# A decoder layer on one core: squares of token group 2 moved into the down stage, first loads and last output in smaller parts, late weight loads reordered

## The chip, the cores and the metric

The kernel runs on one core of a Trainium2 chip. The core has five engines with instruction queues of their own: TensorE (PE: matmuls; its weight loads are shown apart as PEld), VectorE (DVE), ScalarE (ACT), GpSimd (POOL) and SyncE (SP), which here issues nearly all DMAs. Each engine works through its queue in order and waits on semaphores for the others. TensorE writes to the eight banks of PSUM; DVE and ACT read them and so make them free again. The metric is the time of one execution in microseconds (us), the median of several runs. All durations below come from one profiled execution.

## What is computed

One layer of a decoder for 1024 prompt tokens and 32 decode tokens, D = 1024, all in float32. Cut to what matters:

```python
h = rms(x, n_mix_pre)
z = h @ w_in                                  # q | k | v | pooling input
mix = concat(attention(z), pooling(z)) @ w_out
x = x + rms(mix, n_mix_post)
f = rms(x, n_ffn_pre)
f = (silu(f @ w_gate) * (f @ w_up)) @ w_down  # 2816 hidden channels
x = x + rms(f, n_ffn_post)
x = x + sigmoid(x @ w_ple_gate) * (p @ w_ple) # the output y
```

`rms(a, g)` is `a * rsqrt(mean(a*a) + eps) * g` over the 1024 channels.

## The kernel before

**Tiles.** The 1056 tokens are three groups (0, 1, 2) of 352. Channels lie on the 128 partitions, tokens on the columns; the 1024 channels are 8 chunks `m` of 128. Almost every matmul is 128x128 weights against 128x352 columns.

**Precision by pairs.** Each float32 operand is split into a rounded high part and the rest: ACT casts (`wh`, `qh`, `sh`, L167), DVE subtracts (`wl`, `ql`, `sl`, L168). `gemm` (L367) makes three matmuls of each product: high by high, high by low, low by high. So TensorE can use no weight before ACT and then DVE have split it. The pairs of weights share the eight slots of `w_tile` (L180); raw weights have three slots, tag "wr" (`W_RAW`, L52); everything as large as half a group lives in 28 activation slots (`act_tile`, L110, `A_SLOTS`); small results such as `sg`, `yo`, `u3` have five slots (`tmp`, L133).

**Seven products instead of eight.** Groups 0 and 1 are multiplied together by Strassen's scheme: sums of weight blocks (POOL, L328 for the down weights, L1128 in `w_sums` for the others) meet sums of activations. Group 2 is multiplied directly. The sums overwrite the raw weights, so the plain split of a raw tile has to come before its sums.

**The order.** TensorE's instructions keep the order in which the program text issues them (`mm`, L124). The other engines' instructions are put in order by the planner of the framework, by their place in the text and by when it reckons them ready; `fix`, `order` and `load` pin single ones. Weights are made ready ahead of use: `need(k)` (L330) walks a list `ITEMS`, makes what is up to `LOOK` = 4 items ahead (split, or sums and split) but none from `until[0]` on, and asks for the raw weights of the next two items by `w_load` (L172).

**Side chains.** Norms run as generators beside the matmuls. `turn(n)` (L972) counts matmuls; `chain(steps, wait)` (L985) lets a generator make its first step `wait` matmuls later, and further steps as the counter passes the times that the generator's own loads set. `rstd_steps` (L391) turns a sum of squares `acc` into a broadcast 1/rms, with six small matmuls, a square root on ACT, a few DVE operations and two matmuls. `ple_steps(g)` (L1332) loads `p` and the saved residual `x1d`, runs `rstd_steps(acc3[g], 28)`, scales, adds and splits the result for the last stage.

**The stages the change touches.**
- Start: `u_load`, `x_load` (L458 on) issue the first weights and x on SP; `u_split`, `x_operand` split them; `u_prod` multiplies, for all four weight tiles first half of the channels, then second half. `x_squares` and `sum_halves` make the sum of squares of x, and `rstd_steps` of group 0 comes after the eighth `u_prod`.
- Output projection: `out_attn(m, g)` for the first four chunks and `out_proj(m, g)` for the last four (groups 0 and 1 here; group 2 is done). `ffn_steps(2)` (L995) is chained ahead of them and makes group 2's norm, residual sum, second norm and operand for the hidden layers. `turn(12)` stands behind each `out_attn`, `turn(24)` behind each `out_proj`.
- Down: `gate_up` and `down` (L1210) run over the hidden slabs; after the last slab `downs(LAST2, (0, 1))` makes the last eight down products of group 2 and, behind each, `finished(m, 2)` (L1233): square on ACT, add into `acc3[2]` on DVE, scale by the gain on ACT. Then `down7(n)` (L1257) runs 19 steps of the Strassen products of groups 0 and 1; each of the steps 0 to 11 is 48 matmuls. `ple_steps(2)` is chained in front of the first step with `wait` 110.
- Last stage: `ple_out(m, 2)` for group 2, then for groups 0 and 1 `ple_first(a)` for a = 7, 5, 3, 1 (a first product, kept as `p1` by ACT, L1443, then a second onto the same bank) and `ple_rest(a, b)` for the pairs (1,0), (3,2), (5,4), (7,6): products with one "half" item and one "sums" item of weights each, added by DVE (L1454). `ple_end` (L1406) makes sigmoid (ACT, L1410), product and sum (DVE, L1412, L1414) and stores the output on SP (L1415).

Of the kernel before, what the change touches and what calls it, by code (L numbers as in the profile page):

```python
# [10 lines left out]
F32 = mybir.dt.float32  # L11
F32R = mybir.dt.float32r
AF = mybir.ActivationFunctionType
# [12 lines left out]
N = T // G  # L26
# [35 lines left out]
def trunk_kernel(  # L62
# [43 lines left out]
    def nm(s):  # L106
        cnt[0] += 1
        return f"{s}{cnt[0]}"
# [4 lines left out]
    def half(g, dt=F32, s="h"):  # L113
        return act_tile([P, 4, NS[g]], dt, s)
# [54 lines left out]

    raws, pairs = {}, {}  # L170

    def w_load(j):  # L172
        if j >= len(plan) or j in raws:
            return
        src, shape = plan[j]
        t = wpool.tile(shape, F32, tag="wr", bufs=W_RAW, name=nm("wr"))
        nc.sync.dma_start(t, src)
        raws[j] = t

# [267 lines left out]
    def load(dst, src):  # L447
        tc.keep_in_program_order(nc.sync.dma_start(dst, src))
# [18 lines left out]
    def x_operand(g, h, behind=False):  # L467
        t = xr[g, h]
        hi, lo = half(g, F32R), half(g, F32R)
        for c in range(4):  # L470
            gc = gn[:, 0, 4 * h + c : 4 * h + c + 1]
            fix(se.activation(hi[:, c, :], t[:, c, :], AF.Identity, scale=gc))  # L472
# [4 lines left out]
        xs[g][h] = hi, lo  # L477

    def x_squares(g):
        sqs = [xr[g, h] for h in range(2)]  # L480
# [2 lines left out]
        acc1[g] = sum_halves(sqs, g)  # L483


    def u_load(c, h):
        j = U0[c]
        if h == 0:
            shape = plan[j][1]
            raws[j] = act_tile(shape) if c == 3 else wpool.tile(shape, F32, tag="wr", bufs=W_RAW, name=nm("wr"))  # L490
        load(raws[j][:, 4 * h : 4 * h + 4, :], plan[j][0][:, 4 * h : 4 * h + 4, :])

    def u_split(c, h):
        j = U0[c]
        if h == 0:
            pairs[j] = w_tile(plan[j][1], "wh"), w_tile(plan[j][1], "wl")
        split(*(t[:, 4 * h : 4 * h + 4, :] for t in pairs[j]), raws[j][:, 4 * h : 4 * h + 4, :])

    u_load(0, 0)
    x_load(0, 0, 2)  # L500
    for c in range(1, 4):
        u_load(c, 0)
    x_load(0, 1)
# [874 lines left out]
    for k in OPERAND.values():  # L1378
        spill(k, len(SETS) - 1)
    share[0] = 0.3  # L1380
    chain(ple_steps(2), 110)
    for n in range(len(STEPS) - 2):
        down7(n)
    finish(list(chains))

    early = {}
# [16 lines left out]
        se.copy(v, embed(wp, m, g))  # L1403
        early[m, g] = v

    def ple_end(gate, wp, m, g):  # L1406

        pp = early.pop((m, g)) if (m, g) in early else embed(wp, m, g)
        sg = tmp(N, "sg")
        se.activation(sg, gate, AF.Sigmoid)  # L1410
        xm = x2[g][m // 4][:, m % 4, :]
        ve.tensor_tensor(sg, sg, pp, op=ALU.mult)  # L1412
        yo = tmp(N, "yo")
        ve.tensor_tensor(yo, sg, xm, op=ALU.add)  # L1414
        nc.sync.dma_start(y_o[:, m, OFF[g] : OFF[g + 1]], yo)  # L1415

    def ple_out(m, g):
        wp, w = WPE[0][m]
# [30 lines left out]
    def ple_rest(a, b):  # L1449
        wp, w, js = W2[a]  # L1450
        p1 = p1s[0][:, a // 2, :]

        def add(out, x, ps):
            ve.tensor_tensor(out, x, ps, op=ALU.add)  # L1454
# [24 lines left out]
    chain(ple_steps(0), 84)  # L1479
    down7(len(STEPS) - 2)  # L1480
# [9 lines left out]
    for a, b in zip(firsts, firsts[1:] + [()]):  # L1490
# [4 lines left out]
        list(a)  # L1495
    finish(list(chains))
    for a, b in PAIRS:
        ple_rest(a, b)
# [86 lines left out]
```

## Time and profile before

| | us |
|---|---|
| median of 3 runs | 1093.62 (1093.57 to 1094.39) |
| profiled execution | 1093.46 |
| its span, first to last instruction | 1091.7 |
| POOL adding down weights, L328, 44 instructions | 72.9 |
| POOL adding other weights, L1128, 52 instructions | 78.9 |

How to read the rows: the view of waits has engine, line, whom it waited for, then us in total, times, and the longest. A row of windows has the window's limits and length, then each engine's busy time with its count of instructions, the granted TensorE clock (1.00 is full), the share of the time in which the 16 DMA engines were busy, and GB/s. A row of the timeline has start, duration, engine, line, operation, output<-inputs, shapes and count; behind it in brackets stands how long the engine had been idle before and who ended that. A row of groups has the count, then busy time, mean ns of one, and idle time before them. Tile names carry no numbers, so "p" is `p1`, "sh" the high part of a sum of weights, "st" a staged activation, "xo" one that is loaded back.

### The profile page before, as it was taken

Reading aid. Unit: us, or ns where it says so; the run is one execution under the profiler, and the core shown is the slowest. Engines: PE = TensorE matmul, PEld = TensorE weight load, DVE = VectorE, ACT = ScalarE, POOL = GpSimd, SP = SyncE. Lnnn points to the kernel's source line nnn. Section 1 sums busy time; section 2 is a strip of 40 time slices with the busy share of each in tenths; the row PEclk is TensorE's granted clock in tenths of the full one; section 3 lists DMA queues with packets and bytes.
Section 4 is the critical chain, followed back from the end, with each engine's and each line's share of the span. In section 5 each row is a group of like instructions: output and inputs, shape, how many; then the busy total and the mean of one; then the engine's idle time right before and its main releaser. Section 6 shows DMA issues by size and latency. Waiting matters only on the chain.

```text
span 1091.7 us, 17619 instructions
## 1 busy us (share of the span) xinstructions
PE 1076.9 (99%) x6867; PEld 1058.8 (97%) x6867; DVE 822.1 (75%) x1277; ACT 512.0 (47%) x921; POOL 279.3 (26%) x213
## 2 busy tenths in 40 slices
PE   9999999999999999999999999999999999999997
PEld 8999988899999999999999999999998999999996
DVE  6766378976888966867758758659669767999877
ACT  8322277764555534344334434435356532575442
POOL 1045023200000042322423223242409085200242
PEclk9999999999999999999999999999999999999998
DMA  8121211352543312342441523515777855837241
GB/s 295 59 71 39 95 61 40 131 226 69 205 172 116 120 54 68 141 184 84 142 180 58 209 112 111 229 39 184 286 261 300 334 176 180 316 116 235 85 148 61
DMA packets 54452, 163.60 MB, mean 150 GB/s; under 512 B 5828, under 2 KB 20068, under 8 KB 54368
## 3 DMA queue, kind: packets, MB, share of 16 engines
q1 hardware_dynamic: 53040, 160.70, 41.8%
q10 hardware_dynamic: 1328, 1.77, 0.5%
q8 instruction: 54, 0.88, 0.3%
q14 instruction: 30, 0.25, 0.1%
HBM read 124.59 MB, written 37.86 MB: 149 GB/s over the span
## 4 chain that ended last, share of the span: by engine, by line
PE 93%; DVE 3%; ACT 1%; issue 1%; DMA 1%; POOL 0%; ACTq 0%; SPq 0%; DVEq 0%; POOLq 0%
PE b L126 93%; PE b L120 1%; DMA xr<-in_x_dram 0%; POOL wr L1128 0%; ACT a L742 0%; DVE yo L1414 0%; DMA wr<-in_w_in_dram 0%; ACT wh L167 0%; DVE u L1329 0%; DVE sg L1412 0%; DVE p L1454 0%; DVE wl L168 0%; DVE ql L168 0%; DVE st L168 0%; DVE u L1454 0%
## 5 line engine op out<-in xcount | busy, mean ns | idle before, releaser
L126 PE MATMUL b<-fh,wh 128*128 128x352 f32 x712 | 229.9, 323 | 0.7 <-ACT p L1443 0.7
L126 PE MATMUL b<-fh,wl 128*128 128x352 f32 x712 | 228.3, 321 | 0.0
L126 PE MATMUL b<-fl,wh 128*128 128x352 f32 x712 | 228.1, 320 | 0.0
L1128 POOL TENSOR_TENSOR wr<-wr 128x512 f32<-128x512 f32 x52 | 78.9, 1517 | 561.2 <-DVE wl L168 275.8
L168 DVE TENSOR_TENSOR wl<-wr,wh 128x1024 fp32r<-128x1024 f32 (+1 forms) x125 | 164.2, 1315 | 57.5 <-ACT wh L167 56.4
L167 ACT CAST wh<-wr 128x1024 fp32r<-128x1024 f32 (+1 forms) x125 | 128.2, 1028 | 153.1 <-PE b L126 98.6
L126 PE MATMUL b<-xo,qh 128*128 128x352 f32 x616 | 147.4, 322 | 0.5 <-DVE o L1225 0.5
L126 PE MATMUL b<-fh,sh 128*128 128x352 f32 x416 | 135.0, 325 | 2.0 <-DVE p L1454 2.0
L126 PEld LDWEIGHTS b<-fh,wh 128*128 128x128 f32 x712 | 133.5, 188 | 1.0 <-ACT p L1443 1.0
L126 PEld LDWEIGHTS b<-fl,wh 128*128 128x128 f32 x712 | 133.9, 188 | 0.0
L126 PE MATMUL b<-fh,sl 128*128 128x352 f32 x416 | 133.8, 322 | 0.0
L126 PE MATMUL b<-fl,sh 128*128 128x352 f32 x416 | 133.8, 322 | 0.0
L126 PEld LDWEIGHTS b<-fh,wl 128*128 128x128 f32 x712 | 133.4, 187 | 0.3 <-DVE wl L168 0.2
L126 PEld LDWEIGHTS b<-xo,qh 128*128 128x128 f32 x616 | 106.6, 188 | 0.8 <-DVE o L1225 0.8
L126 PE MATMUL b<-h,wh 128*128 128x352 f32 x480 | 105.7, 326 | 1.3 <-ACT h L472 0.9
L126 PE MATMUL b<-xo,ql 128*128 128x352 f32 x308 | 99.4, 323 | 2.0 <-DVE ql L168 1.9
L168 DVE TENSOR_TENSOR sl<-wr,sh 128x1024 fp32r<-128x1024 f32 x52 | 63.4, 1220 | 42.3 <-ACT sh L167 42.2
L328 POOL TENSOR_TENSOR wq<-wq,wq 128x512 f32<-128x512 f32 x44 | 72.9, 1695 | 71.3 <-DVE ql L168 60.1
L126 PEld LDWEIGHTS b<-h,wh 128*128 128x128 f32 x480 | 82.5, 190 | 2.2 <-ACT h L472 1.1
L126 PE MATMUL b<-hid,wh 128*128 128x352 f32 x352 | 84.1, 322 | 0.0
L167 ACT CAST sh<-wr 128x1024 fp32r<-128x1024 f32 x52 | 53.6, 1049 | 63.0 <-POOL wr L1128 59.1
L167 ACT CAST st<-c 128x352 fp32r<-128x352 f32 x55 | 26.7, 487 | 117.6 <-DVE c L1199 96.7
(202 smaller groups left out, 2176.6 us busy)
## 6 DMA issues: line engine op xcount, KB each, us to landing
wr<-in_w_gu_dram SPq DMA_DIRECT2D x64, 512.0 KB, 3.4
xd<-st SPq DMA_DIRECT2D x35, 704.0 KB, 4.5
xo<-xd SPq DMA_DIRECT2D x35, 704.0 KB, 6.0
wr<-in_w_dn_dram SPq DMA_DIRECT2D x22, 512.0 KB, 3.5
wq<-in_w_dn_dram SPq DMA_DIRECT2D x20, 512.0 KB, 8.9
wr<-in_w_pg_dram SPq DMA_DIRECT2D x18, 512.0 KB, 3.9
x<-in_x_dram SPq DMA_DIRECT2D x6, 704.0 KB, 9.0
x1d<-x SPq DMA_DIRECT2D x6, 704.0 KB, 3.6
```

Of the source, the lines that this page charges most:

```text
L120: ins = te.transpose(out, src, ident)
L126: ins = te.matmul(*args, **kw)
L167: fix(se.copy(hi, src))
L168: fix(ve.tensor_tensor(lo, src, hi.bitcast(F32), op=ALU.subtract))
L328: ge.tensor_tensor(*(q_load(q, e)[:, i, :] for q in (out, a, b)), op=op)
L1128: ge.tensor_tensor(out, a, b, op=op)
```

## The change

1. First loads: the first chunk (of eight) of the first w_in tile is a transfer of its own, then the first chunk of x, then chunks 1 to 3 of the weights, then x in one and two chunks. It was four chunks of weights, then x by two and two. The splits follow the same parts.
2. `finished(m, 2)` is no longer called behind each last down product, but two at a time after `down7(2)` to `down7(5)`; `ple_steps(2)` is chained after step 5 with `wait` 40.
3. In the last stage `until[0]` is set to the first "sums" item, so that none is made before the last `ple_first` has begun; at that point it is lifted, and the raw weights of the three later pairs are asked for at once, those of the last two pairs into activation slots.
4. The norm chain of group 2 ahead of the hidden layers, `ffn_steps(2)`, is chained with `wait` 16, where it was 8.
5. `ple_end` can work in parts: the last output adds, takes the sigmoid, multiplies, adds and stores in two halves of 176 columns.

```diff
-    def w_load(j):
+    def w_load(j, home=None):
...
-        t = wpool.tile(shape, F32, tag="wr", bufs=W_RAW, name=nm("wr"))
+        t = home(shape) if home else wpool.tile(shape, F32, tag="wr", bufs=W_RAW, name=nm("wr"))
...
-    def x_load(g, h, n=1):
+    def x_load(g, h, parts=(4,), behind_first=None):
         xr[g, h] = half(g, s="xr")
-        for c in range(0, 4, 4 // n):
-            cs = slice(c, c + 4 // n)
-            k = slice(4 * h + c, 4 * h + c + 4 // n)
-            load(xr[g, h][:, cs, :], x[:, k, OFF[g] : OFF[g + 1]])
+        c = 0
+        for n in parts:
+            load(xr[g, h][:, c : c + n, :], x[:, 4 * h + c : 4 * h + c + n, OFF[g] : OFF[g + 1]])
+            if c == 0 and behind_first:
+                behind_first()
+            c += n
...
-    u_load(0, 0)
-    x_load(0, 0, 2)
+    u_part(0, slice(0, 1))
+    x_load(0, 0, (1, 1, 2), lambda: u_part(0, slice(1, 4)))
...
-    u_split(0, 0)
-    x_operand(0, 0)
+    u_split(0, 0, slice(0, 1))
+    x_operand(0, 0, cs=range(1))
+    u_split(0, 0, slice(1, 4))
+    x_operand(0, 0, cs=range(1, 4))
...
-    chain(ffn_steps(2), 8, alone=True)
+    chain(ffn_steps(2), 16, alone=True)
...
                 down(n, m)
-                if n == LAST2:
-                    finished(m, 2)
...
-    chain(ple_steps(2), 110)
     for n in range(len(STEPS) - 2):
         down7(n)
+        if 2 <= n < 6:
+            for m in (2 * n - 4, 2 * n - 3):
+                finished(m, 2)
+        if n == 5:
+            chain(ple_steps(2), 40)
...
-    def ple_end(gate, wp, m, g):
+    def ple_end(gate, wp, m, g, parts=1, into=None):
...
+        n = N // parts
+        for i in range(0, N, n):
+            v = slice(i, i + n)
+            if into is not None:
+                ve.tensor_tensor(into[:, v], into[:, v], gate[:, v], op=ALU.add)
+            se.activation(sg[:, v], (gate if into is None else into)[:, v], AF.Sigmoid)
+        for i in range(0, N, n):
+            v = slice(i, i + n)
+            ve.tensor_tensor(sg[:, v], sg[:, v], pp[:, v], op=ALU.mult)
+            ve.tensor_tensor(yo[:, v], sg[:, v], xm[:, v], op=ALU.add)
+            nc.sync.dma_start(y_o[:, m, OFF[g] + i : OFF[g] + i + n], yo[:, v])
...
-        if not early_s4:
-            add(p1, p1, product(s["S4"], e7["B22"]))
-        ple_end(p1, wp, a, 1)
+        if early_s4:
+            ple_end(p1, wp, a, 1)
+        else:
+            ple_end(product(s["S4"], e7["B22"]), wp, a, 1, parts=2, into=p1)
...
     finish(chains[:-1])
+    until[0] = W2[1][2]
     firsts = [ple_first(a) for a in (7, 5, 3, 1)]
...
         if not b:
+            until[0] = len(ITEMS)
+            for a, _ in PAIRS[1:]:
+                for j in ITEMS[W2[a][2]][1]:
+                    w_load(j, act_tile if a > 4 else None)
             for m in range(4):
                 embed_early(W1[1][0], m, 1)
```

The `u_part` helper loads any chunks of a w_in tile, and `u_split` and `x_operand` take the chunks to split.

More of the change, by code (lines that the diff above doesn't have):

```diff
@@ L456, in trunk_kernel, with x_operand @@
     xr = {}
-    def x_load(g, h, n=1):
+    def x_load(g, h, parts=(4,), behind_first=None):
         xr[g, h] = half(g, s="xr")
-        for c in range(0, 4, 4 // n):
-            cs = slice(c, c + 4 // n)
-            k = slice(4 * h + c, 4 * h + c + 4 // n)
-            load(xr[g, h][:, cs, :], x[:, k, OFF[g] : OFF[g + 1]])
+        c = 0
[4 more added lines that the diff above has]
+            c += n
     xs, acc1, r1 = [[None] * 2 for _ in range(G)], [None] * G, [None] * G
-    def x_operand(g, h, behind=False):
+    def x_operand(g, h, behind=False, cs=range(4)):
         t = xr[g, h]
-        hi, lo = half(g, F32R), half(g, F32R)
-        for c in range(4):
+        hi, lo = xs[g][h] = xs[g][h] or (half(g, F32R), half(g, F32R))
+        for c in cs:
             gc = gn[:, 0, 4 * h + c : 4 * h + c + 1]
@@ L483, in x_squares, with u_part, u_load, u_split @@
         acc1[g] = sum_halves(sqs, g)
-    def u_load(c, h):
+    def u_part(c, ks):
         j = U0[c]
-        if h == 0:
+        if j not in raws:
             shape = plan[j][1]
             raws[j] = act_tile(shape) if c == 3 else wpool.tile(shape, F32, tag="wr", bufs=W_RAW, name=nm("wr"))
-        load(raws[j][:, 4 * h : 4 * h + 4, :], plan[j][0][:, 4 * h : 4 * h + 4, :])
-    def u_split(c, h):
+        load(raws[j][:, ks, :], plan[j][0][:, ks, :])
+    def u_load(c, h):
+        u_part(c, slice(4 * h, 4 * h + 4))
+    def u_split(c, h, part=slice(0, 4)):
         j = U0[c]
-        if h == 0:
+        ks = slice(4 * h + part.start, 4 * h + part.stop)
+        if j not in pairs:
             pairs[j] = w_tile(plan[j][1], "wh"), w_tile(plan[j][1], "wl")
-        split(*(t[:, 4 * h : 4 * h + 4, :] for t in pairs[j]), raws[j][:, 4 * h : 4 * h + 4, :])
-    u_load(0, 0)
-    x_load(0, 0, 2)
+        split(*(t[:, ks, :] for t in pairs[j]), raws[j][:, ks, :])
+    u_part(0, slice(0, 1))
+    x_load(0, 0, (1, 1, 2), lambda: u_part(0, slice(1, 4)))
     for c in range(1, 4):
@@ L1404, in embed_early @@
         early[m, g] = v
-    def ple_end(gate, wp, m, g):
+    def ple_end(gate, wp, m, g, parts=1, into=None):
         pp = early.pop((m, g)) if (m, g) in early else embed(wp, m, g)
-        sg = tmp(N, "sg")
-        se.activation(sg, gate, AF.Sigmoid)
         xm = x2[g][m // 4][:, m % 4, :]
[L1412 to L1415, printed above, removed]
+        sg, yo = tmp(N, "sg"), tmp(N, "yo")
+        n = N // parts
[9 more added lines that the diff above has]
+            nc.sync.dma_start(y_o[:, m, OFF[g] + i : OFF[g] + i + n], yo[:, v])
     def ple_out(m, g):
@@ L1487, in trunk_kernel @@
     finish(chains[:-1])
+    until[0] = W2[1][2]
     firsts = [ple_first(a) for a in (7, 5, 3, 1)]
     next(firsts[0])
-    for a, b in zip(firsts, firsts[1:] + [()]):
+    for gen, b in zip(firsts, firsts[1:] + [()]):
         list(zip(range(1), b))
         if not b:
+            until[0] = len(ITEMS)
+            for a, _ in PAIRS[1:]:
+                for j in ITEMS[W2[a][2]][1]:
+                    w_load(j, act_tile if a > 4 else None)
             for m in range(4):
                 embed_early(W1[1][0], m, 1)
-        list(a)
+        list(gen)
     finish(list(chains))
```

1 line of the change is left out of this document (removed).

## The prediction

> **What bounds the kernel now.** I read the page's head first, then TensorE's own waits (engine, whom it waited for, us in total, times, longest), then the windows around the stalls.
>
> ```profile
> span 1091.7 us, 17619 instructions
> PE 1076.9 (99%) x6867; PEld 1058.8 (97%) x6867; DVE 822.1 (75%) x1277; ACT 512.0 (47%) x921; POOL 279.3 (26%) x213
> ```
> ```profile
> PE b L126 <- DVE p L1454: 2.0, 1, 2.0
> PE b L126 <- DVE ql L168: 1.9, 1, 1.9
> ...
> PE b L126 <- DVE acc L892: 0.7, 1, 0.7
> PE b L126 <- ACT p L1443: 0.7, 1, 0.7
> PE b L126 <- DVE o L1225: 0.5, 1, 0.5
> ```
> ```profile
> core 0: us, PE busy (x) PEld busy (x) DVE busy (x) ACT busy (x) POOL busy (x), PEclk, DMA share, GB/s
> ...
> 836.10:838.20 2.10, 0.18 (x3) 0.01 (x1) 2.10 (x2) 2.10 (x4) 0.95 (x1) 1.00 1.01 418
> 1072.40:1074.40 2.00, 0.02 (x1) 0.02 (x1) 1.97 (x5) 0.91 (x2) 0.00 (x0) 1.00 0.02 4
> 1075.76:1079.18 3.42, 3.42 (x13) 3.13 (x13) 3.28 (x7) 0.99 (x2) 0.00 (x0) 0.50 0.16 58
> ```
>
> TensorE is busy 99% of the span, and the change neither adds nor removes a matmul. So only time in which TensorE stands still or runs at a lower clock can be won: the start, five stalls, and what follows the last matmul. The stalls are 0.7 us at 223 (for DVE's add into acc), 1.9 us at 836 (for ql, the low half of a down weight), 0.7 us at 1037 (ACT's copy of p), 2.0 us at 1072 (DVE's add into p) and 0.5 us at 821 (DVE's add into o). The 1072 stall costs twice: 2.0 us idle, then a stretch of 3.42 us at a granted clock of 0.50, half of which, 1.7 us, is lost.
>
> The Trainium skill, "TensorE: Matmul & The Clock Gate", section "Why this matters for your kernels", says that the clock falls after gaps of over about 3 us. The trace disagrees: 2.0 us did it here at 1072, while 1.9 us at 836 did not (1.00).
>
> **Finer first loads.** The w_in tile's first chunk and x's first chunk come as transfers of their own, so the first matmul can start earlier. What limits the stage is elsewhere.
>
> ```profile
> 7.39:10.80 3.41, 3.41 (x12) 3.40 (x13) 2.26 (x5) 2.13 (x5) 0.00 (x0) 0.50 1.05 369
> ```
> ```profile
> 13.75 2.03 ACT L472 ACTIVATE h<-xr,c 128x352 fp32r<-128x352 f32 x4 [0.56 <-DMA xr<-in_x_dram]
> ...
> 18.00 1.37 ACT L482 ACTIVATE xr<-xr 128x1408 f32<-128x1408 f32 x1
> ```
> ```profile
> 21.44 0.89 DVE L438 TENSOR_TENSOR xr<-xr 128x704 f32<-128x704 f32 x1
> ...
> 22.74 0.52 DVE L440 TENSOR_TENSOR acc<-xr 128x352 f32<-128x352 f32 x1
> ```
> ```profile
> 23.45 0.80 PEld L126 LDWEIGHTS b<-c,acc 128*128 128x128 f32 x6
> ```
>
> TensorE's order is fixed, and after the first 96 products it needs acc of group 0. That sum ends at 22.74 + 0.52 = 23.26, and TensorE takes it at 23.45 without a wait: 0.2 us of slack. The sum hangs on ACT, which starts x of group 1 when its DMA lands (13.75, after a wait) and then works through to the squares (18.00 + 1.37). The DMA engines are full meanwhile (share 1.05), and the bytes stay the same. So TensorE may start nearly 1 us earlier and will wait for acc at 23. Bounds: 0.2 us won (the slack), 0.9 lost if the two added issues, some 0.45 us each, push the landing out in full. I take 0, because the full DMA engines set the landing.
>
> **Norm of group 2 ahead of the hidden layers.** `chain(ffn_steps(2), ...)` waits 16 matmuls for 8.
>
> ```profile
> 223.04 0.52 DVE L892 TENSOR_TENSOR acc<-acc,sq 128x352 f32<-128x352 f32 x1
> ```
>
> TensorE stood 0.7 us until this add had ended, at 223.56. The counter moves by 12 for each `out_attn`, so the norm's first matmuls come one `out_attn` later: 12 matmuls, 1.9 us, more than the stall. **The 0.7 us go.** Next is the add of another group's sum, which that `out_attn` doesn't need. The chain isn't later behind it: from 12 its steps fall due at 36, 72 and 105, from 24 at 48, 84 and 117, and the counter, which moves by 24 from 96 on, meets 105 and 117 at the same 120. Bounds: 0 and 0.7.
>
> **Squares of group 2 spread.** `finished(m, 2)` leaves the last down products (eight times an ACT square, a DVE add into acc, an ACT scale) and comes two at a time after steps 2 to 5.
>
> ```profile
> L892 DVE TENSOR_TENSOR acc<-acc,sq 128x352 f32<-128x352 f32 x7 | 9.2, 1316 | 0.2
> L168 DVE TENSOR_TENSOR ql<-wq,qh 128x1024 fp32r<-128x1024 f32 x4 | 7.9, 2022 | 0.0
> ```
> ```profile
> L1240 ACT ACTIVATE o<-o,c 128x352 f32<-128x352 f32 x7 | 3.9, 582 | 0.0
> ...
> L891 ACT ACTIVATE sq<-o 128x352 f32<-128x352 f32 x7 | 3.4, 496 | 4.7 <-DVE o L1225 4.6
> ```
>
> These are DVE's and ACT's groups from 819 to 841, where DVE has no idle time. Out go 9.2 us of DVE and 3.9 + 3.4 us of ACT, ahead of the ql that TensorE waits for: the **1.9 us at 836 go**. What is late next is ql itself, with 9 us now free in front of it. Afterwards each of the four steps, some 7.5 us of matmuls, takes two adds (1.0 to 2.6 us of DVE) and 2.2 us of ACT; I cost that at nothing, since the old norm chain leaves these steps at the same time. The 0.5 us at 821 stay: DVE's splits of st stand ahead of that add, and they don't move.
>
> **Last norm of group 2 later.** `ple_steps(2)` starts 328 matmuls after the down stage's begin, where it started after 110, so some 35 us later. All its instructions move: on SP two loads of p and two of x1d, on ACT a table load, on DVE the scaling.
>
> ```profile
> 840.00:850.00 10.00, 10.00 (x67) 10.00 (x66) 9.90 (x11) 6.42 (x11) 6.42 (x4) 1.00 1.02 417
> ...
> 878.80:905.70 26.90, 26.90 (x171) 26.90 (x170) 19.32 (x21) 6.11 (x7) 26.90 (x16) 1.00 0.58 192
> ```
> ```profile
> 850.48 3.14 DVE L1347 TENSOR_TENSOR o<-o,b 128x1408 f32<-128x1408 f32 x2
> 853.54 1.62 DVE L1348 TENSOR_TENSOR x<-x,o 128x1408 f32<-128x1408 f32 x1
> ...
> 860.18 1.63 DVE L168 TENSOR_TENSOR fl<-x,fh 128x1408 fp32r<-128x1408 f32 x1 [1.22 <-ACT fh L167]
> ...
> 877.46 1.23 DVE L168 TENSOR_TENSOR ql<-wq,qh 128x1024 fp32r<-128x1024 f32 x1 [0.41 <-PE b L126]
> ```
> ```profile
> L168 DVE TENSOR_TENSOR ql<-wq,qh 128x1024 fp32r<-128x1024 f32 x7 | 13.2, 1893 | 4.4 <-ACT qh L167 3.0 <-PE b L126 1.4
> ```
>
> Here the change moves work from where POOL idles to where POOL sums weights without a pause (878.8 to 905.7, 26.90 of 26.90). A ql there took 1893 ns against 1230 alone, 1.54 times. The chain's DVE work becomes 3.14 + 2 x 1.62 x 1.54 + 2 x 1.63 x 1.54 = 13.2 us, where DVE has 26.9 - 19.3 = 7.6 us free: 5.6 us too many, with ql queued behind them. Bounds: 0 (in 840 to 850 DVE was 99% busy beside POOL and TensorE lost nothing) and 5.6 us lost. I take **0.8 us lost**, near the first row, since ql is split a step ahead. On SP the four loads meet xo loads that run a step or more ahead: nothing.
>
> The Trainium skill, "SBUF — State Buffer", section "Who interferes with whom", says that a DVE instruction with two SBUF inputs and a GpSimd instruction that reads SBUF block each other. The trace agrees (1893 against 1230 ns). It speaks against this edit, and is the mechanism of the second rival.
>
> **Tail weights.** `until` keeps the first weight sums (pair 1, 0) from being emitted before the last `ple_first` has begun, and the raw weights of the last two pairs go to activation slots, not to the three raw slots.
>
> ```profile
> 1036.37 1.05 ACT L167 CAST sh<-wr 128x1024 fp32r<-128x1024 f32 x1 [6.38 <-POOL wr L1128]
> 1037.32 0.45 ACT L1443 COPY p<-b 128x352 f32<-128x352 f32 x1
> ...
> 1050.76 0.62 ACT L167 CAST w<-wr 128x512 fp32r<-128x512 f32 x1 [1.93 <-DMA wr<-in_w_pg_dram]
> ```
> ```profile
> 1053.84 2.82 POOL L1128 TENSOR_TENSOR wr<-wr,wr 128x512 f32<-128x512 f32 x2 [0.37 <-DMA wr<-in_w_pg_dram]
> ```
> ```profile
> 1047.55 1.59 SPq L177 DMA_DIRECT2D wr<-in_w_pg_dram  x2
> ...
> 1060.57 0.33 SPq L177 DMA_DIRECT2D wr<-in_w_pg_dram  x1
> ```
> ```profile
> 1059.31 1.23 DVE L168 TENSOR_TENSOR sl<-wr,sh 128x1024 fp32r<-128x1024 f32 x1 [2.27 <-ACT sh L167]
> ...
> 1071.61 1.23 DVE L168 TENSOR_TENSOR sl<-wr,sh 128x1024 fp32r<-128x1024 f32 x1 [2.26 <-ACT sh L167]
> ```
>
> At 1037 the copy of p stands in ACT's queue behind a cast that waited 6.38 us for POOL; with the sums emitted later the copy comes first, and the **0.7 us go**. At 1072 DVE stood 2.26 us before sl, the split of the last sums, with the add into p that frees TensorE's bank queued behind it. Those sums are late because the chain is: load, cast, split, POOL sums, cast, split, for each pair; and the loads came only when raw slots came free (1047.55 and 1060.57). Asked for around 1030, they are there some 10 us early, the cast at 1050.76 loses its 1.93 us and POOL can follow on from one pair to the next. If the chain gains about 2.3 us, the **2.0 us at 1072 go and with them the 1.7 us of half clock**. Next is DVE's queue, which still has 2.27 us of idle time before 1059.31 in hand. Bounds: nothing, if hand-offs and not loads set the chain, and 3.7 us. I take all of it, for the loads' waits stand in the chain's own rows. New waits: the last two of the six loads wait for a slot (I count 25 of 28 activation slots in use when four more are asked for) and stores queue behind them on SP; a held store keeps one of the five `tmp` tiles, for which DVE would wait next. Until about 1040 other tiles cover that.
>
> **Last output in halves.**
>
> ```profile
> 1086.66 0.51 DVE L1454 TENSOR_TENSOR p<-p,b 128x352 f32<-128x352 f32 x1
> 1087.73 0.52 DVE L1412 TENSOR_TENSOR sg<-sg,b 128x352 f32<-128x352 f32 x1 [0.56 <-ACT sg L1410]
> 1088.29 0.53 DVE L1414 TENSOR_TENSOR yo<-sg,x 128x352 f32<-128x352 f32 x1
> ```
>
> From add to output it takes 1088.82 - 1086.66 = 2.16 us. A DVE operation of 704 columns took 0.89 us and one of 352 took 0.52, so one of 176 takes about 0.33. The path becomes an add, a sigmoid (about 0.35) and four DVE operations: 0.33 + 0.35 + 4 x 0.33 = 2.0 us. **0.2 us go**; bounds 0.5 won, 0.3 lost to hand-offs and the second store.
>
> **Sum.** 0 - 0.7 - 1.9 + 0.8 - 0.7 - 2.0 - 1.7 - 0.2 = -6.4 us. The profiled execution took 1093.46 us with its 1.8 us around the span, 0.2 below the median 1093.62, so the forecast is 1087.1 us.
>
> **Rivals.**
> - The tail's chain is set by hand-offs, or the early loads find no slot and come no earlier. Then TensorE waits again at 1072 for what it won at 1037: -0.7 - 1.9 + 0.8 - 0.2 = -2.0, or 1091.5; in part, 1089.5. For it: POOL's sums and four hand-offs per pair remain. Against: the 1.93 and 0.37 us for loads. 0.20.
> - The moved norm chain collides with POOL's sums from 878 to 906. It decides from the point where DVE's lag passes the 2.1 us that it has free in a step (7.6 us in 3.6 steps). In full: 5.6 us of stalls for ql and two stretches of half clock, 3.4 us, against 7.2 won (the sum without its 0.8), so 1.8 us slower: 1095.3. One more stretch of half clock makes it 1097. For it: 5.6 us too many. Against: the window from 840. In full 0.09; half of it, with the tail's gain, 1089.5: 0.08.
> - A 2 us gap costs no clock, as the skill's page on the clock gate has it. The 1072 stall is then worth 2.0 alone: 1088.8. The row at 0.50 speaks against it. 0.03.
>
> **Chances.** Forecast (1084.5 to 1089) 0.60, rivals as given. Faster by over 0.2%, which is about what can be told from no change here (below 1091.4): 0.60 + 0.08 + 0.03 and 0.08 of the first rival, 0.79; same 0.12; slower 0.09. The range reaches from 1084.5 (no collision, 0.8; the halves' and the start's better ends, 0.5; the rest from DVE's idle time in the tail) to 1091.5, the first rival, and leaves out the collision in full.
>
> **What would show it.** Right: no wait of TensorE for acc near 223 or ql near 836, none for ACT's copy of p, none for DVE's p, no 0.50 clock near the end, and a wait for acc near 23. Wrong: stalls for ql between 875 and 910, sl still waiting 2 us for sh, stores held behind loads on SP, or a start that is over 0.5 us earlier at 26.

## The result, and the profile after

The changed kernel takes 1098.36 us (median of 6 runs, 1097.12 to 1098.77), the kernel before took 1094.44 beside it (6 runs): a ratio of 1.0029, with a 95% interval from 1.0016 to 1.0043. The forecast was 1087.1 and faster; the change made the kernel slower by some 3 us. The profiled execution took 1098.62 us; it and the one before lie further apart than the medians do. In the changed code the add into acc stands in L899, the operand of x in L474, the add into p in L1469, POOL's other sums in L1135.

First the head of the page after, then TensorE's own waits (us in total, times, longest), then windows around its stalls.

```profile
span 1096.8 us, 17629 instructions
...
PE 1079.4 (98%) x6867; PEld 1060.0 (97%) x6867; DVE 828.0 (75%) x1281; ACT 512.3 (47%) x923; POOL 279.1 (25%) x213
```
```profile
PE b L126 <- DVE ql L168: 4.3, 3, 1.7
PE b L126 <- ACT h L474: 2.0, 2, 1.3
PE b L126 <- DVE p L1469: 1.9, 1, 1.9
...
PE b L126 <- DVE dg L415: 0.7, 2, 0.5
PE b L126 <- DVE fl L168: 0.6, 1, 0.6
PE b L126 <- DVE o L1232: 0.5, 1, 0.5
```
```profile
core 0: us, PE busy (x) PEld busy (x) DVE busy (x) ACT busy (x) POOL busy (x), PEclk, DMA share, GB/s
837.90:839.90 2.00, 0.35 (x3) 0.15 (x2) 2.00 (x2) 1.21 (x2) 0.83 (x2) 1.00 1.02 408
894.30:896.90 2.60, 1.57 (x9) 0.99 (x7) 2.60 (x3) 2.36 (x3) 2.60 (x2) 1.00 0.56 169
904.40:906.40 2.00, 0.43 (x3) 0.14 (x1) 2.00 (x2) 0.13 (x1) 2.00 (x2) 1.00 0.25 104
...
1077.80:1079.90 2.10, 0.29 (x2) 0.00 (x0) 2.07 (x5) 1.13 (x2) 0.00 (x0) 1.00 0.01 4
1080.93:1084.34 3.41, 3.41 (x13) 3.41 (x12) 3.27 (x6) 0.75 (x2) 0.00 (x0) 0.50 0.16 58
```

The waits for acc and for ACT's p are gone. The wait for ql, one of 1.9 us before, is now three of 4.3 together: the old one (near 838) stayed, and two came near 895 and 904. The stall for p, now at 1078, still has 1.9 us, and the half clock behind it is still there. The waits for h at the start grew from 0.9 to 2.0 us, and the wait for fl near 1044 is new.

To say where the 5.1 us between the two spans came from, I took the distance between the starts of neighbouring products of 352 columns, less the usual 0.159, and summed it over each stage: the start +2.3 us, the norm ahead of the hidden layers -0.5, the stall at 836 -0.3, 879 to 907 +3.6, the tail +0.2 (0.7 won near 1037, 0.9 lost near 1044), and the end behind the last matmul -0.3. That is +5.0, and 11.4 us from the forecast's -6.4: the tail makes 4.6 of it, the last norm of group 2 2.8, the start 2.3, the squares 1.6. Stalls of TensorE are given in this way below too, at the start of the last product ahead of them.

### The profile page after: what moved, and what is told of

It is laid out like the page before. It is cut to its first block, busy times and chain, and to the rows that moved or that the text cites. A ratio compares the mean times of both kernels' runs of the same rounds, so it can differ in the third digit from the quotient of the medians.

```text
span 1096.8 us, 17629 instructions
## 1 busy us (share of the span) xinstructions
PE 1079.4 (98%) x6867; PEld 1060.0 (97%) x6867; DVE 828.0 (75%) x1281; ACT 512.3 (47%) x923; POOL 279.1 (25%) x213
## 4 chain that ended last, share of the span: by engine, by line
PE 86%; DVE 5%; issue 3%; POOL 2%; ACT 2%; DMA 1%; SPq 0%; POOLq 0%; ACTq 0%; DVEq 0%
PE b L126 86%; DVE ql L168 2%; POOL a L1135 1%; POOL wr L1135 1%; PE b L120 1%; DMA xr<-in_x_dram 1%; DMA a<-in_w_pg_dram 1%; DVE acc L899 0%; DVE u L1300 0%; ACT a L749 0%; DMA wr<-in_w_in_dram 0%; DVE o L1354 0%; DVE o L1232 0%; DVE dg L409 0%; DVE x L1355 0%
## 5 line engine op out<-in xcount | busy, mean ns | idle before, releaser
L1135 POOL TENSOR_TENSOR wr<-wr 128x512 f32<-128x512 f32 x48 | 71.3, 1486 | 551.0 <-DVE wl L168 275.8
L168 DVE TENSOR_TENSOR wl<-wr,wh 128x1024 fp32r<-128x1024 f32 (+2 forms) x126 | 164.2, 1305 | 56.0 <-ACT wh L167 55.6
L167 ACT CAST wh<-wr 128x1024 fp32r<-128x1024 f32 (+2 forms) x126 | 128.4, 1021 | 150.4 <-PE b L126 98.4
L168 DVE TENSOR_TENSOR sl<-wr,sh 128x1024 fp32r<-128x1024 f32 x48 | 58.5, 1220 | 37.2 <-ACT sh L167 37.2
L167 ACT CAST st<-c 128x352 fp32r<-128x352 f32 x55 | 26.7, 487 | 117.5 <-DVE c L1206 96.6
L126 PEld LDWEIGHTS b<-fh,sh 128*128 128x128 f32 x416 | 78.6, 189 | 2.2 <-issue 2.2
```

What stands on the lines that cost most here:

```text
L126: ins = te.matmul(*args, **kw)
L167: fix(se.copy(hi, src))
L168: fix(ve.tensor_tensor(lo, src, hi.bitcast(F32), op=ALU.subtract))
L1135: ge.tensor_tensor(out, a, b, op=op)
```

## The experiments

All are compared with runs of the kernel before on the same chip; ratios are this to before.

### The change in four pieces

The diffs are pieces of the one shown above. The start alone:

```diff
-    u_load(0, 0)
-    x_load(0, 0, 2)
+    u_part(0, slice(0, 1))
+    x_load(0, 0, (1, 1, 2), lambda: u_part(0, slice(1, 4)))
```

> Before plus the finer first loads, weight split and first operand alone. Theory (the extra loads make every later load of the start land later, by 1.5 to 2.1 us in the changed kernel): the norm matmul of group 0 comes 2.0 to 2.4 us later than in the kernel before (it stood at 26.46 us there, at 28.80 in the changed one) and the time is 1.9 to 2.4 us longer. Rival (the later landings belong to that one profile, by chance or by another part of the change): the norm matmul within 0.3 us of 26.46 and the time within 0.5 us of before. The prediction's own value for this part was 0, with bounds of -0.2 and +0.9.

Measured: 1.0018 (1.0009 to 1.0028), 2.0 us; norm matmul at 28.88, 2.4 us later. So the later landings belong to this edit; whether the number of loads makes them is tested further on.

The squares and the last norm of group 2 alone:

```diff
-                if n == LAST2:
-                    finished(m, 2)
...
-    chain(ple_steps(2), 110)
...
+        if 2 <= n < 6:
+            for m in (2 * n - 4, 2 * n - 3):
+                finished(m, 2)
+        if n == 5:
+            chain(ple_steps(2), 40)
```

> Before plus the squares of group 2 and its last norm moved, alone. Theory (the planner puts the squares back where they were, so the stall for ql near 836 stays; the norm's scaling and adds meet POOL's dsum differences at 879 to 906): the stall at 836 keeps 1.7 to 2.1 us, new waits for ql between 885 and 910 cost 3 to 4 us, and the time is 2.8 to 3.6 us longer. Rival, the prediction's steps: stall at 836 gone (-1.9), collision +0.8, time 1.1 us shorter. Second rival (the new waits come from the start's shift and not from the moved norm): stall stays, no wait for ql in 885 to 910, time within 0.5 us.

Measured: 1.0024 (1.0011 to 1.0037), 2.6 us. TensorE's stalls were 1.80 at 836.4, 1.14 at 894.2 and 1.72 at 903.2. The theory holds in kind: the old stall stayed and the new waits came. Their sum, 2.86, and the time lie just under its ranges.

The tail alone:

```diff
+    until[0] = W2[1][2]
...
+            until[0] = len(ITEMS)
+            for a, _ in PAIRS[1:]:
+                for j in ITEMS[W2[a][2]][1]:
+                    w_load(j, act_tile if a > 4 else None)
```

> Before plus the tail's loads ahead of the stores and its bounded look-ahead, alone. Theory (hand-offs between ACT, DVE and POOL set the chain of the last weight sums, not the loads, and the four early loads hold activation slots): the 0.7 us stall near 1037 goes, a stall of 0.7 to 0.9 us for fl comes some 8 us later, the gap of 2.1 us near 1072 stays with the clock at half for 3.4 us behind it, and the time is within 0.4 us of before. Rival, the prediction's steps: stall near 1037 gone, gap and half clock gone, time 4.4 us shorter.

Measured: 0.9996 (0.9987 to 1.0006). By the distances between products the stall near 1037 is gone, 0.64 us for fl came at 1039.4 (smaller and earlier than expected), and 1.90 stayed at 1072.9. The half clock behind it did not come this time, which neither theory said; the last section tells why.

The two pieces that worked:

```diff
-    chain(ffn_steps(2), 8, alone=True)
+    chain(ffn_steps(2), 16, alone=True)
...
-        ple_end(p1, wp, a, 1)
+            ple_end(product(s["S4"], e7["B22"]), wp, a, 1, parts=2, into=p1)
```

> Before plus the two parts that seem to have worked: the ffn norm of group 2 started 16 instead of 8 units later, and the last output in halves. Theory and prediction agree: 0.5 to 0.7 us from the first (the stall for acc near 223 goes, a wait of 0.2 for dg may come behind it) and 0.2 to 0.4 from the second, so 0.7 to 1.1 us shorter. Rival (the parts' gains in the changed kernel belong to its shifted times): within 0.3 us of before.

Measured: 0.9986 (0.9976 to 0.9995), 1.5 us shorter, above the expected 0.7 to 1.1, which the interval holds. The profile shows 0.7 us less at 223 to 229.

The four ratios multiply to 1.0024, within the interval of the whole change. That agrees with pieces that act by themselves, within an interval of 1.4 us either way, and each can be looked into alone.

### The start: number of transfers, or small ones first?

Two runs split the start's edit, and two more vary x alone.

```diff
-    u_load(0, 0)
-    x_load(0, 0, 2)
+    u_part(0, slice(0, 1))
+    x_load(0, 0, (2, 2), lambda: u_part(0, slice(1, 4)))
```
That is the run with the weights in pieces. The other three load the weights whole, as before, and x as `(1, 1, 2)`, `(2, 1, 1)` and `(4,)`. The expectations stand in the order x in 1, 1 and 2, weights in pieces, x in 2, 1 and 1, x whole; the last two were written when the first two had been measured.

> Before with the first half of x of group 0 loaded in parts of 1, 1 and 2 chunks instead of 2 and 2; the weights are loaded and split whole, as before. Theory A (each further transfer of the list holds the later ones up by its issue on SP, 0.45 us): the norm matmul of group 0 about 0.5 us later than the 26.5 to 26.9 of the kernels with the old start, time 0.3 to 0.6 us longer. Theory B (the single chunks of x make the transfers slow): norm matmul 1.5 to 2.3 us later, time 1.5 to 2.3 us longer. Theory C (the weight pieces make them slow): norm matmul within 0.3 us, time within 0.3 us.

> Before with the first weight's first half loaded and split as one chunk of 64 KB and then three of 192 KB, the three behind the first part of x; x in parts of 2 and 2 as before. Theory A (issue on SP, 0.45 us for a transfer): norm matmul about 0.5 us later, time 0.3 to 0.6 us longer. Theory B (single chunks of x): norm matmul within 0.3 us, time within 0.3 us. Theory C (the weight pieces): norm matmul 1.5 to 2.3 us later, time 1.5 to 2.3 us longer.

> Before with the first half of x of group 0 in parts of 2, 1 and 1 chunks (1, 1 and 2 in the run before, 2 and 2 in the kernel before). Theory N (the number of transfers lowers the rate): 1.75 to 1.9 MB between 3 and 9 us, time 0.7 to 1.8 us longer than before. Theory F (small transfers at the very front lower it): 2.0 MB or more, time within 0.5 us of before.

> Before with the first half of x of group 0 in one transfer of four chunks. Theory N (number of transfers): 2.1 MB or more between 3 and 9 us, the norm matmul of group 0 no later than 26.5, time 0.3 to 1 us shorter than before. Theory F (small first transfers): bytes as before, 2.0 to 2.1 MB; time within 0.5 us, since the first product waits for more and the full transfers set the norm matmul.

| first loads | ratio (interval) | moved from 3 to 9 us | norm matmul at |
|---|---|---|---|
| old start, 10 profiles | | 2.00 to 2.11 MB | 26.3 to 26.8, once 27.9 |
| change's start | 1.0018 (1.0009 to 1.0028) | 1.67 MB | 28.9 |
| x 1, 1, 2 | 1.0016 (1.0006 to 1.0026) | 1.82 MB | 27.0 |
| weights 1, 3 | 1.0002 (0.9992 to 1.0013) | 1.97 MB | 26.7 |
| x 2, 1, 1 | 1.0001 (0.9992 to 1.0011) | 2.09 MB | 26.4 |
| x 4 | 1.0009 (0.9999 to 1.0020) | 2.16 MB | 27.8 |

One more transfer costs nothing where it comes behind a larger one (x 2, 1, 1): theory N falls, and with it the weight of theory A. The run with x in 1, 1 and 2 had A's place of the norm matmul with B's time, and settles neither. A single chunk of x at the front loses 0.2 to 0.3 MB, a single chunk of weights at most 0.1, both together 0.3 to 0.4. The run with x whole moves most, but its first product waits until 6.77 us and nothing is won; its time, 1.0 us longer with an interval from -0.1 to 2.2, fits neither theory. In single profiles the two pieces don't add up either: x in 1, 1 and 2 moved the norm matmul by some 0.5 us, the weights by 0.3 at most, both by 2.4. Why the transfers move fewer bytes behind a small first one was not found; and the profile of x 1, 1, 2 shows only some 0.5 us of its ratio's 1.7 at the norm matmul, and has two stretches of half clock before the last matmul where the kernel before has one, so the size of that piece's cost is less sure than its sign.

### The squares of group 2, moved in fact

```diff
-            se.activation(sq, src, AF.Square)
+            fix(se.activation(sq, src, AF.Square))
...
-    share[0] = 0.3
-    chain(ple_steps(2), 110)
+    share[0] = 0.6
     for n in range(len(STEPS) - 2):
         down7(n)
+        if 1 <= n < 3:
+            fixed[0] = True
+            for m in range(4 * n - 4, 4 * n):
+                finished(m, 2)
+            fixed[0] = False
+        if n == 2:
+            chain(ple_steps(2), 6)
```

> Before with the squares of group 2 really moved: each is held behind the last PSUM copy of a down product on ScalarE, four behind product 1 and four behind product 2, and the norm chain starts after product 2 with its share of VectorE at 0.6 instead of 0.3, so that it ends before POOL's differences begin at 879. Theory (in the change the squares were not moved, and it is they that hold ql back at 836): the stall of 2.1 us at 836 and the half clock of 0.6 behind it go, no wait for ql between 879 and 910, time 1.8 to 2.6 us shorter. Rival (ql at 836 waits for its quarter buffer or for POOL's differences, which run until 837, and not for the squares): stall of over 1.5 us stays, time within 0.6 us of before, or longer where the shorter norm chain crowds the copies.

Measured: 1.0051 (1.0039 to 1.0063), slower. The stall at 836 was gone, but TensorE stood 5.1 us at 845.6 for DVE's acc: TensorE's order is fixed, and the norm's sum stood in it ahead of the last squares. That is a fault of the experiment's own wait, so the next one changed only it (6 to 40). The 6.4 us in its expectation count the sum's six small matmuls too.

> As the kernel with the pinned squares, but the norm chain starts 40 instead of 6 units after product 2, so that its sum over partitions no longer stands on TensorE ahead of the last square. In the kernel before this one the stall at 836 was gone and one of 6.4 us came at 845.6, on the sum itself. Theory (the squares hold ql back at 836, and a norm chain that neither comes early nor meets POOL costs nothing): no stall at 836, none at 845 to 880 over 0.3 us, no wait for ql between 879 and 910, time 1.8 to 2.6 us shorter than before. Rival (the shorter chain, at twice the share of VectorE, crowds the splits of ql): stalls of together over 1.5 us between 855 and 880, time within 0.6 us of before or longer.

Measured: 0.9975 (0.9966 to 0.9984), 2.7 us shorter. This is the timeline of DVE, then a window where the old stall was.

```profile
828.31 3.86 DVE L168 TENSOR_TENSOR ql<-wq,qh 128x1024 fp32r<-128x1024 f32 x2 [1.39 <-ACT qh L167]
836.04 4.35 DVE L168 TENSOR_TENSOR ql<-wq,qh 128x1024 fp32r<-128x1024 f32 x2 [3.88 <-ACT qh L167]
840.32 4.68 DVE L892 TENSOR_TENSOR acc<-acc,sq 128x352 f32<-128x352 f32 x3
```
```profile
836.10:838.20 2.10, 2.10 (x15) 2.10 (x14) 2.10 (x2) 2.07 (x4) 2.10 (x2) 1.00 0.02 7
```

DVE now waits for work (1.39 and 3.88 us of idle time), the adds come behind ql, and TensorE is busy throughout this window. By the distances between products 2.1 us were won here, as the theory had it. The rest of the profile moved as well, which the theory did not have: a wait of 1.1 us for wl came at 976.7, and the stall at 1037 (0.9) and the half clock near 1075 did not come. So 2.1 us is the price of the squares' place, and 2.7 that of the whole run.

### The late norm alone

```diff
-    chain(ple_steps(2), 110)
+    chain(ple_steps(2), 310)
```

> Before with one number changed: the chain of the last norm of group 2 starts 310 instead of 110 units on, which moves its scaling and adds from 847 to 877 into about 879 to 909, where POOL's differences run; the squares stay where they are. Theory (the collision of the late norm with POOL is what costs, not the move of the squares): waits for ql of together 3 to 4 us between 885 and 912, the stall of 2.1 us at 836 stays, time 2.8 to 3.8 us longer. Rival (it is the squares' new place that costs): no new wait for ql, time within 0.5 us of before.

Measured: 1.0034 (1.0023 to 1.0045), 3.7 us longer: the price of the theory. Its form was another: one stall, of 1.98 us at 910.1, with a stretch of half clock behind it, and not several waits for ql. These are POOL's differences, TensorE going on behind the stall, DVE's ql ahead of it, and windows at the stall and the half clock.

```profile
879.82 31.04 POOL L328 TENSOR_TENSOR wq<-wq,wq 128x512 f32<-128x512 f32 x16 [33.70 <-DVE ql L168]
```
```profile
912.19 0.56 PE L126 MATMUL b<-xo,qh 128*128 128x352 f32 x2 [1.82 <-ACT fh L167]
```
```profile
909.68 2.26 DVE L168 TENSOR_TENSOR ql<-wq,qh 128x1024 fp32r<-128x1024 f32 x1
```
```profile
910.10:912.20 2.10, 0.28 (x3) 0.04 (x1) 2.10 (x2) 1.89 (x2) 0.76 (x1) 1.00 0.99 392
913.42:916.83 3.41, 3.41 (x13) 3.41 (x12) 2.08 (x3) 0.00 (x0) 0.00 (x0) 0.50 1.05 412
```

The profile puts the stall down to ACT's fh; but this ql ends at 909.68 + 2.26 = 911.94, a quarter of a microsecond before TensorE goes on, so which of the two held it is open. POOL's 16 differences took 31.04 us, against 26.90 in the window of before: the two engines hold each other up.

### The tail's hand-offs

The loads early, the next pair's half weight split ahead of the current pair's sums, and the last half weight in an activation slot (`EARLY` is 3 and 5):

```diff
-        W2[a] = wp0, item("half", jb), item("sums", ja, jb)
+        todo.append((a, wp0, item("half", jb), ja, jb))
+        if len(todo) > 1:
+            sums_item()
+    sums_item()
...
     finish(list(chains))
+    until[0] = len(ITEMS)
+    for a in EARLY:
+        for j in ITEMS[W2[a][2]][1]:
+            w_load(j, act_tile)
```

> Before with the bounded look-ahead of the tail kept, the next pair's half weight split ahead of the current pair's sums (so that POOL's sums no longer wait for a VectorE split that is queued behind the previous sums' split), the weights of the second and third pair loaded into activation slots only after the last operand is made, and the last half in an activation slot. Theory (the hand-offs POOL, ACT, DVE, POOL of 12.3 to 12.6 us a pair set the tail): POOL's gaps of 5 to 6.6 us in front of the second and third pair's sums shrink below 2 us, the stall of 2.1 us near 1072 and the half clock behind it go, no new stall for fl over 0.3 us near 1040, time 2.5 to 4 us shorter. Rival (the loads set it, or the weights' slots: a sum's split then waits for the previous pair's products): the stall near 1072 stays above 1.5 us, time within 1 us of before.

Measured: 1.0003 (0.9994 to 1.0012). The stall at 1072 was gone, in its place stood 2.58 us at 1037.0 and 1.42 at 1067.7. Neither theory: the hand-off was gone, and the gain went to two others. ACT's queue shows the first.

```profile
1038.33 1.04 ACT L168 CAST sh<-wr 128x1024 fp32r<-128x1024 f32 x1 [8.09 <-POOL wr L1138]
1039.28 0.45 ACT L1453 COPY p<-b 128x352 f32<-128x352 f32 x1
```

The copy that frees TensorE's bank stands behind a cast that waits 8.09 us for POOL. The next run writes the first sums into the program ahead of the embedding products, and holds their first split behind that copy and POOL's sums in their order.

```diff
+            until[0] = W2[1][2] + 1
+            need(W2[1][2])
...
+        fixed[0] = tail and not held
         split(*hl, src)
```

> As the kernel with the tail's reordered halves, and the first sums' split held behind the last copy of p on ScalarE, POOL's sums held in their order. In the kernel before this one POOL's gaps were gone and the stall at 1072 with them, but the copy of p at 1039 stood behind that split (2.6 us at 1037) and 1.4 us came at 1067.7, on a split that is queued behind the output's products on VectorE. Theory (each gain of the tail is taken by the next hand-off in ScalarE's and VectorE's order): the stall at 1037 goes below 0.9 us, the one near 1067 stays between 1 and 2, no half clock before 1080, time 1.0 to 2.5 us shorter than before. Rival (loads or slots): a stall above 1.5 us at 1037 or a new one of over 1.5 us at 1045 to 1060, time within 0.6 us of before.

Measured: 0.9972 (0.9963 to 0.9981), 3.1 us shorter. Nothing is left at 1037 or 1072; 0.68 us stands at 1061.7 and 1.03 at 1066.3, both for sl. The theory holds, the gain is above its range: no half clock came near the end but the one after the last matmul.

### What gained, together

The two pieces that worked, the held squares and the tail with held splits, with the old start:

> The parts that gained, together: the ffn norm of group 2 at 16, the last output in halves, the squares held behind the copies of products 1 and 2 with the norm chain 40 units after product 2, and the tail with reordered and held splits; the start as before. Theory (the parts lie in different stages and add up): 0.9986 x 0.9975 x 0.9972 = 0.9933 of before, 7.3 us shorter, with no stall near 836 and 1037, 0.7 us less at 223, and only one stretch of half clock, at the end. Rival (the stalls share their half clocks, or the tail shifts against POOL when the earlier parts move it): one of the gains is missing, 4 to 6 us shorter, with a stall above 1.5 us somewhere after 1040.

Measured: 0.9932 (0.9920 to 0.9945), 1087.86 us against 1095.01, faster than both kernels. The parts add up as their ratios said (0.9933), within 1.4 us either way. Both the squares' run and the tail's had lost the 0.9 us at 1037, which the sum counts twice, and that is too little to be told in this interval.

## Why the prediction was wrong, step by step

**Finer first loads: 0 forecast, 2.0 us lost.** The failed step is "I take 0, because the full DMA engines set the landing", with the bound of 0.9 that counted only two issues. This is the view of DMA from 3 to 9 us, before and then after, and the norm matmul after; then the third and fourth chunk of x on ACT, before and after.

```profile
DMA packets 1380, 2.07 MB, mean 345 GB/s; under 512 B 88, under 2 KB 992, under 8 KB 1380
```
```profile
DMA packets 1115, 1.67 MB, mean 279 GB/s; under 512 B 104, under 2 KB 749, under 8 KB 1115
```
```profile
28.80 0.56 PE L126 MATMUL b<-dg,c 128*128 128x352 f32 x2 [0.48 <-DVE dg L415]
```
```profile
6.08 1.07 ACT L472 ACTIVATE h<-xr,c 128x352 fp32r<-128x352 f32 x2 [0.18 <-DMA xr<-in_x_dram]
```
```profile
8.20 1.07 ACT L474 ACTIVATE h<-xr,c 128x352 fp32r<-128x352 f32 x2 [1.76 <-DMA xr<-in_x_dram]
```

A busy DMA engine isn't a fixed rate: the busy share of the 16 engines from 3 to 9 us went from 1.00 to 0.93, the bytes down by a fifth. 0.4 MB less in 6 us is 1.2 us at 345 GB/s. ACT starts the two chunks 2.1 us later (8.20 less 6.08), so 0.9 us stay unexplained; the two added issues, 0.45 us each, would make them, but in the run with x in 2, 1 and 1 an added issue cost nothing. TensorE does start nearly 1 us earlier, as forecast, and then waits for the operand h, not for acc.

**Norm of group 2: -0.7 forecast, -0.5 measured.** The wait for acc is gone. A quarter of a microsecond came back at 231, ahead of the norm's matmul with dg: the distance between the starts there is 0.39 us, for the usual 0.159. The view of waits doesn't list it; its second wait for dg, at 52, was there before. That is the norm's own chain, which the step had as no later.

**Squares spread: -1.9 forecast, -0.3 measured.** The failed step is "Out go 9.2 us of DVE". They did not go out. This is the timeline of DVE before, in part, and then after.

```profile
831.64 4.27 DVE L892 TENSOR_TENSOR acc<-acc,sq 128x352 f32<-128x352 f32 x3
835.84 7.90 DVE L168 TENSOR_TENSOR ql<-wq,qh 128x1024 fp32r<-128x1024 f32 x4
```
```profile
826.91 1.80 DVE L1232 TENSOR_TENSOR o<-o,b 128x352 f32<-128x352 f32 x4
828.63 8.83 DVE L899 TENSOR_TENSOR acc<-acc,sq 128x352 f32<-128x352 f32 x6
837.39 3.44 DVE L168 TENSOR_TENSOR ql<-wq,qh 128x1024 fp32r<-128x1024 f32 x2
```

Six of the seven adds still stand ahead of the ql for which TensorE waits. The change moved the place in the program where the squares are written; the order of ACT's and DVE's instructions is the planner's, which places each when its inputs are ready. Only TensorE's order and what is held by `fix` are bound to the program. I had read the diff as if it were the order on the engine. That the squares do hold ql back, the other half of the step, was right: held in their new place, they gave the 2.1 us of this stall.

**Last norm later: +0.8 forecast, +3.6 measured.** The mechanism was right and its size off: the term stood between 0 and 5.6, and I took the lower row. These are groups of DVE from 879 to 907 after, with the count, busy time and mean ns, and the same lines from 848 to 877 in the run with the held squares.

```profile
L168 DVE TENSOR_TENSOR ql<-wq,qh 128x1024 fp32r<-128x1024 f32 x6 | 11.9, 2001 | 3.9 <-ACT qh L167 3.9
...
L1355 DVE TENSOR_TENSOR x<-x,o 128x1408 f32<-128x1408 f32 x2 | 4.7, 2335 | 0.0
L1354 DVE TENSOR_TENSOR o<-o,b 128x1408 f32<-128x1408 f32 x2 | 3.2, 1607 | 0.0
```
```profile
L168 DVE TENSOR_TENSOR ql<-wq,qh 128x1024 fp32r<-128x1024 f32 x8 | 10.6, 1351 | 3.5 <-ACT qh L167 2.5 <-PE b L126 1.0
...
L1348 DVE TENSOR_TENSOR x<-x,o 128x1408 f32<-128x1408 f32 x2 | 3.2, 1618 | 0.0
L1347 DVE TENSOR_TENSOR o<-o,b 128x1408 f32<-128x1408 f32 x2 | 3.2, 1618 | 1.7 <-PE b L126 1.7
```

The splits ql and the adds of x and o take 1.4 to 1.5 times as long beside POOL (2001 against 1351 ns, 2335 against 1618). The operation of the same size that reads one input from PSUM (`b`) does not: 1607 against 1618. The window from 840 to 850, on which the 0.8 rested, was no match: POOL was busy for 6.42 of its 10 us only. The Trainium skill, "SBUF — State Buffer", section "Who interferes with whom", has DVE and GpSimd block each other; the trace agrees in both directions (2335 against 1618 ns on DVE, 31.04 against 26.90 us on POOL). This was the second rival, at some two thirds of its 5.6 us of stalls and without its half clock.

**Tail weights: -4.4 forecast, +0.2 in the changed kernel, 0.9996 alone.** The failed step is "I take all of it, for the loads' waits stand in the chain's own rows". The loads did come early, and POOL began no earlier against TensorE. These are POOL's rows before and after, then ACT's after.

```profile
1052.18 1.29 POOL L1128 TENSOR_TENSOR wr<-wr 128x512 f32<-128x512 f32 x1 [5.74 <-DVE w L168]
...
1064.78 1.29 POOL L1128 TENSOR_TENSOR wr<-wr 128x512 f32<-128x512 f32 x1 [6.58 <-DVE w L168]
```
```profile
1058.06 1.30 POOL L1135 TENSOR_TENSOR a<-a 128x512 f32<-128x512 f32 x1 [5.02 <-DVE w L168]
...
1070.38 1.29 POOL L1135 TENSOR_TENSOR a<-a 128x512 f32<-128x512 f32 x1 [6.58 <-DVE w L168]
```
```profile
1053.08 2.00 ACT L167 CAST sh<-wr 128x1024 fp32r<-128x1024 f32 x2 [3.86 <-POOL wr L1135]
1054.98 0.62 ACT L167 CAST w<-a 128x512 fp32r<-128x512 f32 x1
```

The cast of the half weight had its data, and stood in ACT's queue behind the casts of the sums before it, which waited for POOL; POOL then waited for DVE's w. The period is 12.3 us (1070.38 less 1058.06), hardly less than the 12.6 before (1064.78 less 1052.18). That was the first rival; a wait for a load that ends inside a longer wait is worth nothing. And the 1.7 us of half clock are no fixed part of this stall, as the last section shows.

The 0.7 us at 1037 went, but not by the step "the copy comes first". These are ACT's rows after, then POOL's first sum before and after.

```profile
1040.01 2.00 ACT L167 CAST sh<-wr 128x1024 fp32r<-128x1024 f32 x2 [4.70 <-POOL wr L1135]
1041.91 0.44 ACT L1458 COPY p<-b 128x352 f32<-128x352 f32 x1
```
```profile
1028.22 3.86 POOL L1128 TENSOR_TENSOR wr<-wr 128x512 f32<-128x512 f32 x1 [92.36 <-DVE w L168]
```
```profile
1033.93 1.45 POOL L1135 TENSOR_TENSOR wr<-wr 128x512 f32<-128x512 f32 x1 [92.89 <-DVE w L168]
```

The copy stands behind two casts that wait for POOL, where it stood behind one. It is in time because POOL's first sum took 1.45 us, for 3.86: before, DVE's split fl of the last operand ran beside it, and after, that split comes only at 1043.66. In all 16 profiles this sum took 3.86 us or more where that split ran beside it, and 1.45 or 1.46 where it didn't. The run with the held squares, with the tail's program as before, lost the stall at 1037 in the same way. So the term's size was right by luck. The same late split is what TensorE waits for at 1044. Why its cast came late is not shown; the run that loads the raw weights only behind the last operand had no such wait, which speaks for the activation slots.

**Last output in halves: -0.2 forecast, -0.3 measured.** From the last add to the end of the last sum it now takes 1.8 us for 2.16, since the two halves overlap by more than I summed.

```profile
1092.27 0.58 DVE L1424 TENSOR_TENSOR p<-p,b 128x176 f32<-128x176 f32 x2
...
1093.51 0.58 DVE L1429 TENSOR_TENSOR yo<-sg,x 128x176 f32<-128x176 f32 x2
```

The 0.5 us at 821 stayed, as forecast. Of the signs named as proof against the forecast, stalls for ql between 875 and 910 and a sl that waits 2 us for sh both came.

## What to carry to other kernels

Ask first who orders the engine: a line moved in the program moves an instruction only where that engine's order is held to the program. In a chain that goes round several engines, a wait for a load that stands in one of its rows is no gain until the hand-offs behind it are shorter; take a hand-off away and look at the next queue at once. Small first transfers can cost more than the earlier start wins, so read the bytes moved and not the share of busy DMA engines.

## What the runs showed of the hardware

Whether a gap of TensorE halves the clock depends on where it falls. In the 16 profiles of before, after and the experiments, the stretches of 0.50 clock ahead of the last matmul are 3.41 us long (one is twice that), and all start at multiples of 3.41 us from one another. I counted these windows back from each run's last such stretch and laid TensorE's 39 gaps of over 1 us behind 250 us, from the distances as above, against them; they put 0.3 us or more of idle time into 55 windows. Where that was 1.98 us or more in one window, the next window was at half clock (12 of 12); where it was 1.96 or less, it was not (0 of 43). The same gap of 2.08 us at 836 split over two windows in the kernel before (0.71 and 1.36 us) and cost no clock, and fell into one in the run with the held splits of the tail (window from 835.8, half clock from 839.2). The prediction had put it down to the gap's length, 2.0 against 1.9 us. A halved window full of matmuls is worth 1.7 us, so executions of a kernel with two gaps of some 2 us can differ by 3.4 us without a difference in the program. The executions on record fit that: of 117 of the kernel before, the 16 with a mean clock of 0.999 took 1094.3 us in the median, the 7 with 0.994 took 1097.3. The Trainium skill, "TensorE: Matmul & The Clock Gate", section "What's actually happening", has an activity window of 3413 ns that runs freely; the trace agrees with that.
